# Hybrid decoder layer: where the decay factors of the SSD groups are formed, and where the memory tiles of the values are loaded and split

## The chip, the cores and the metric

The kernel runs as one program on one core of one Trainium2 chip. The metric is the device time of one execution in microseconds (us); the median of three runs is given.

## The reference

One decoder layer on x (512 positions, 1024 features) with a fixed memory of 256 rows, all in float32: a SwiGLU feed-forward network (hidden width 2816, weight 0.5), a hybrid mixer, cross-attention into the memory with 4 heads, a second feed-forward network, and a norm. The change lies in the mixer and at the beginning of the cross-attention. The mixer has a state-space (SSD) half of 16 heads in 4 groups, and a differential-attention half of 8 heads; both end in one output projection. Cut to what matters:

```python
z, xbc, dt_raw, q, k, v = split_sizes(h @ w_in, IN_SIZES)
xbc = silu(causal_dwconv(xbc, conv_w, conv_b)); xs, bs, cs = split(xbc)
la_cum = cumsum(dt * a) within chunks of 128 positions
decay = exp(where(causal, la_cum[l] - la_cum[s], -inf))
y_diag = einsum('bclsg,bclsgr,bcsgrp->bclgrp', cb, decay, xdt)   # cb = C B^T
y_off  = einsum('bclgn,bcgrpn,bclgr->bclgrp', cc, prev, exp(la_cum))
y = (y_diag + y_off + d_skip * xh) * silu(z)        # then a norm over each group
x = x + concat([y_ssd, y_attn]) @ w_out
v_mem = rms_norm(mem) @ w_cv                        # cross-attention's values
```

## The kernel before

**Products.** Each float32 product of this region is made of three matmuls on split operands: high by high, low by high, high by low. `load_w` loads a weight tile of 128 rows with a DMA on SP's queue (`wr`, 6 buffers), forms its high half on ACT (`wh`, line 155 in `split_into`) and its low half on DVE (`wl`, line 156); both have 3 buffers. PE can use a weight when ACT and then DVE have passed it.

**Order.** The class `Order` (`od`) sets the order in which the program is written. Its list of dense generators (`od.add`) yields after each product; beside them run chains, started by `od.spawn(gen, after)`. A chain goes on when the order's own time `od.t`, which each matmul advances by an assumed cost, has come to its due time; the table `W` (lines 38 to 40) holds the delays that a chain yields between its steps. On PE, DVE and ACT a scheduler puts the instructions in their final order from there; on SP and POOL the order of the program stands.

The dense list in the region is:

```python
    od.add(group_dense(0))
    od.add(out_attn(0, 0, 8))
    od.add(queries_keys(4))
    od.add(values(1))
    ...
    od.add(group_dense(2))
    od.add(group_dense(3))
    od.add(out_attn(1, SPLIT, 8, True))
    od.add(memory_values())
    od.add(out_proj(ys, a["wos"], ...))
```

**Groups.** `group_dense(g)` makes four convolved tiles of a group (products `pxbc`, then `conv` and gating `th2`), starts the chain `group`, and makes two gate tiles (`pz`). The chain of a group makes, with delays between: `pcb` and its masked copy `cbm`; the transpositions of the x tiles (`pxt`, then `xdt` and `xde` on DVE); those of B (`pbt`, copied to `btk` on ACT); the states (`pst`, `st`); and for each pair j of heads a decay block and the products that need it, `pf` (from the states) and `py` (from the decay). A decay block for (group, j) is, for each of two heads, one Exp of 64x512 (line 890), four Relu of 128x128 (892) and one Exp of 128x512 (893) on ACT and a product with `cbm` on DVE (894). It works in place on tiles that `decays` has loaded on ACT's queue; in the profile these are named `gate` for j = 0 and `th` for j = 1. The end of the chain gates with z, forms the norm (`pn` on PE, `nv` on DVE, `ncol` on POOL, `rh`, `ch` and `cl` on DVE), two diagonal tiles `ndiag` on POOL (line 368), their product `nrow`, and `y` (935), split into `ysh` and `ysl`.

**Beside them.** `queries_keys` and `values` make q, k and v of head attention (`pq`, `pk`, `pv`; the key tile is split into `kh` and `kl`). `out_attn` multiplies attention's result (`ya`) by the weights woa, 512 wide, into `pm`, which DVE adds to x. `memory_prep` loads eight tiles of the memory, 128x256, on SP's queue, and splits each (`hm`, line 159 on ACT and 160 on DVE); `memory_values` multiplies them by the weights wcv into four banks `pcv`.

Of the kernel before, what the change touches and what calls it, by code (L numbers as in the profile page):

```python
# [13 lines left out]
AF = mybir.ActivationFunctionType  # L14
ALU = mybir.AluOpType
# [20 lines left out]
LEAD = 4  # L36

W = {"h0": 3.4, "hs": 3.3, "hv": 2.08, "hp": 6.75}
W |= {"g0": 8.28, "gc": 0.75, "gx": 0.92, "gb": 2.59, "gs": 0.51, "gt": 2.0, "gd": 6.9, "gy": 0.38, "gq": 11.02, "gn": 6.52}
W |= {"v": 21.8, "c0": 4.97, "cs": 3.0, "ct": 4.82}  # L40

SPLIT, AHEAD = 5, 2
# [58 lines left out]
def body(tc, a, dbg=None):  # L101
# [13 lines left out]
    def nm(s):  # L115
        uid[0] += 1
        return f"{s}_{uid[0]}"

    def s2(s, dt=F32, shape=(P, T)):
        if math.prod(shape[1:]) <= T // 2:  # L120
            return sp.tile(list(shape), dt, tag="s1", name=nm(s), bufs=NHALF)
        return sp.tile(list(shape), dt, tag="s2", name=nm(s))
# [7 lines left out]
    def acc(s, shape=(P, T)):  # L130
        return acc_p.tile(list(shape), F32, tag="acc", name=nm(s))

    def aux(s, shape=(P, T)):
        return aux_p.tile(list(shape), F32, tag="aux", name=nm(s))
# [6 lines left out]
    V, S, G = nc.vector, nc.scalar, nc.gpsimd  # L141
    od = Order()
# [448 lines left out]
    def col64(s):  # L591
        return cp.tile([P, 4, 16], F32, name=s)

    cum, cdec, dend, dth = col64("cum"), col64("cdec"), col64("dend"), col64("dth")
# [176 lines left out]
        ya[hd] = split("ya", pt, wsub)  # L771
        dump(f"ya_{hd}", ya[hd][0])

    def out_attn(hg, o0, o1, prep=False):
        if prep:
            od.spawn(memory_prep(hm2, 1.5), 4.0)
        yield lambda: all(y is not None for y in ya[4 * hg : 4 * hg + 4])
        heads = ya[4 * hg : 4 * hg + 4]
        for o in range(o0, o1):
            po = acc("pm")  # L780
            yield from proj(po, load_w(a["woa"][hg, o], 4 * P), heads)
            V.tensor_tensor(x[o], x[o], po, ALU.add)
        if o1 == KT:
            ya[4 * hg : 4 * hg + 4] = [None] * 4
# [20 lines left out]
    ys = [None] * 8  # L805

    def group_dense(g):
        bc, xs, zs = [], [], []
        yield from xbc_tile(8 + g, bc)
        yield from xbc_tile(12 + g, bc)  # L810
        for j in range(2):
            yield from xbc_tile(2 * g + j, xs)
        od.spawn(group(g, bc[0], bc[1], xs, zs), W["g0"])
        for j in range(2):
            ps = acc("pz")
            yield from proj(ps, load_w(a["wz"][2 * g + j]), h)
            zs.append(silu2(ps))

    rows_of = {}
# [9 lines left out]
    def group(g, bt, ct, xs, zs):  # L829
        hsl = slice(4 * g, 4 * g + 4)  # L830

        def by_head(t):
            return t.rearrange("p c (h e) -> p c h e", e=64)


        pcb = aux("pcb", (P, 4, P))
        for c in range(4):
            mm(pcb[:, c], bt[:, c * P : (c + 1) * P], ct[:, c * P : (c + 1) * P], True, True)
        cbm = s2("cbm", shape=(P, 4, P))
        V.tensor_tensor(cbm, pcb, triq[:, None, :].to_broadcast([P, 4, P]), ALU.mult)  # L840
        yield W["gc"]
        xdt, xde = [], []
        for c2 in range(2):
            pt = aux("pxt", (P, 2, 256))
            for c in range(2):
                for j in range(2):
                    transpose(pt[:, c, j * P : (j + 1) * P], xs[j][:, (2 * c2 + c) * P : (2 * c2 + c + 1) * P])
            xd = s2("xdt", shape=(P, 2, 256))
            V.tensor_tensor(by_head(xd), by_head(pt), dth[:, 2 * c2 : 2 * c2 + 2, hsl, None].to_broadcast([P, 2, 4, 64]), ALU.mult)
            nc2 = 2 - c2  # L850
            xe = s2("xde", shape=(P, nc2, 256))
            V.tensor_tensor(by_head(xe), by_head(xd[:, :nc2]), dend[:, 2 * c2 : 2 * c2 + nc2, hsl, None].to_broadcast([P, nc2, 4, 64]), ALU.mult)
            xdt.append(xd)
            xde.append(xe)
            yield W["gx"]
        pb = aux("pbt", (P, 3, P))
        for c in range(3):
            transpose(pb[:, c], bt[:, c * P : (c + 1) * P])
        btk = s2("btk", shape=(P, 3, P))
        S.activation(btk, pb, AF.Copy)  # L860
        yield W["gb"]

        st = []
        for c in range(3):
            pst = aux("pst", (P, 256))
            mm(pst, btk[:, c], xde[c // 2][:, c % 2], True, True)
            sc = s2("st", shape=(P, 256))
            if c == 0:
                S.activation(sc, pst, AF.Copy)
            else:  # L870
                V.tensor_tensor(
                    sc.rearrange("p (h e) -> p h e", e=64),
                    st[-1].rearrange("p (h e) -> p h e", e=64),
                    cdec[:, c, hsl, None].to_broadcast([P, 4, 64]),
                    ALU.mult,
                )
                V.tensor_tensor(sc, pst, sc, ALU.add)
            st.append(sc)
            if c < 2:
                yield W["gs"]  # L880
        yz = []
        for j in range(2):
            rs = rows_of.pop((g, j))
            py = aux("py")
            e2 = s2("e2")
            for hh in range(2):
                hd = 4 * g + 2 * j + hh
                pp = slice(64 * hh, 64 * hh + 64)
                r = rs[hh]
                S.activation(e2[pp], r[pp].rearrange("p a b -> p (a b)"), AF.Exp)  # L890
                for c in range(4):
                    S.activation(r[:, c], r[:, c], AF.Relu, bias=cum[:, c, hd : hd + 1], scale=-1.0)
                S.activation(r, r, AF.Exp, scale=-1.0)
                V.tensor_tensor(r, r, cbm, ALU.mult)
            yield W["gd"] + (W["gt"] if j == 0 else 0.0)
            pf = aux("pf")
            with behind(list(newest_mm)):
                for c in range(1, 4):
                    mm(pf[:, c * P : (c + 1) * P], st[c - 1][:, j * P : (j + 1) * P], ct[:, c * P : (c + 1) * P], True, True)
                for c in range(4):  # L900
                    for hh in range(2):
                        pp = slice(64 * hh, 64 * hh + 64)
                        mm(py[pp, c * P : (c + 1) * P], xdt[c // 2][:, c % 2, (2 * j + hh) * 64 : (2 * j + hh + 1) * 64], rs[hh][:, c], True, True)
            if g < 3:
                decays(g + 1, j)
            dsk = dskh[:, 2 * g + j : 2 * g + j + 1]
            V.scalar_tensor_tensor(e2[:, P:], pf[:, P:], 0.5, e2[:, P:], ALU.mult, ALU.mult)
            y = s2("y")
            V.scalar_tensor_tensor(y, xs[j], dsk, py, ALU.mult, ALU.add)
            V.tensor_tensor(y[:, P:], y[:, P:], e2[:, P:], ALU.add)  # L910
            dump(f"y_{2*g+j}", y)
            yz.append(y)
            yield W["gy"]
        while len(zs) < 2:
            yield 1.0
        sq = []
        for j in range(2):
            V.tensor_tensor(yz[j], yz[j], zs[j], ALU.mult)
            q_ = s2("ysq")
            S.activation(q_, yz[j], AF.Square)  # L920
            sq.append(q_)
        G.tensor_tensor(sq[0], sq[0], sq[1], ALU.add)
        yield W["gq"]
        pn = aux("pn", (P, 4))
        for b in range(4):
            mm(pn[:, b : b + 1], sq[0][:, b * P : (b + 1) * P], ones[:, 0:1], True, True)

        rr = inv_rms_cols(pn, 4, 1.0 / (4 * 256), EPS)
        rh = small("rh", 4)
        V.tensor_scalar(rh, rr, 0.5, None, ALU.mult)  # L930
        yield W["gn"]
        pr = row_of(rh, 4, G, G)
        for j in range(2):
            n = 2 * g + j
            V.scalar_tensor_tensor(yz[j], yz[j], par[:, C_SSD + n : C_SSD + n + 1], pr, ALU.mult, ALU.mult)
            ys[n] = split("ys", yz[j])
            dump(f"ys_{n}", ys[n][0])
# [19 lines left out]
    def memory_prep(dst, apart=2.0):  # L957
        mem = [memory_tile(k) for k in range(KT)]
        for k, mk in enumerate(mem):
            with behind(recent):  # L960
                dst.append(split("hm", mk, par[:, C_MEM + k : C_MEM + k + 1], True))
            yield apart
# [69 lines left out]
    hm, hm2 = [], []  # L1032
# [13 lines left out]
    od.add(out_attn(1, 0, SPLIT))  # L1046
    od.add(group_dense(2))
    od.add(group_dense(3))
    od.add(out_attn(1, SPLIT, 8, True))
    od.add(memory_values())  # L1050
    od.add(out_proj(ys, a["wos"], lambda: all(y is not None for y in ys), upd_c))

# [351 lines left out]
```

## Time and profile before

| what | value |
|---|---|
| runs | 1333.7, 1337.35, 1333.83 us; median 1333.83 |
| profiled execution | 1333.16 us, span 1331.4 us |
| mean granted clock of TensorE | 0.996 |
| PE, PEld, DVE busy | 1305.6, 1136.6, 976.2 us |
| ACT, POOL busy | 663.0, 112.3 us |
| instructions | 20052 |

PE is TensorE's matmuls and PEld its weight loads; ACT is ScalarE, DVE is VectorE, POOL is GpSimd, and SP issues DMAs. A shape such as 128x512 is partitions by elements. In rows of the trace the first number is the start in us and the second the duration; "[5.67 <-ACT wh L155]" is idle time of that engine ahead of the instruction and what ended it. The engines and queues work side by side, so a busy engine costs time only where another waits for it.

### The profile page before, as it was taken

To read this page: it belongs to the slowest core of one execution; us is meant where nothing else is said; L and a number is where in the kernel's file an instruction comes from. 1 tells how busy PE (TensorE), PEld (TensorE's weight loads), DVE (VectorE), ACT (ScalarE), POOL (GpSimd) and SP (SyncE) were. 2 spreads that over 40 slices of the span, in tenths; PEclk is the share of its full clock that TensorE was granted. 3 is DMA by queue.
4 is the path that set the end of the run, shared out by engine and by line. 5 is a ranking of instruction groups with operands and counts; after the bars stand their busy time and mean duration, and the time that the engine had idled before them with its cause. 6 is when DMAs were issued, how large, how long until landed. Compare 5 with 4: busy or idle time off the path is not lost. (4 is left out here: it accounts for less than half of the span.)

```text
span 1331.4 us, 20052 instructions
## 1 busy us (share of the span) xinstructions
PE 1305.6 (98%) x7769; PEld 1136.6 (85%) x7769; DVE 976.2 (73%) x1528; ACT 663.0 (50%) x1114; POOL 112.3 (8%) x127
## 2 busy tenths in 40 slices
PE   8999999999999999999999989999999999999997
PEld 7898998899887778777788868888889999989995
DVE  6874778487885786647767776656678878887896
ACT  6442445154453564336644645434455545554564
POOL 0000010000010011200112021120001100000001
PEclk9999999999999999999999999999999999999999
DMA  7444577556464435763276477786239776666762
GB/s 271 111 127 127 127 198 246 134 145 172 128 234 151 126 87 128 225 200 99 60 208 197 109 205 225 200 208 173 61 114 244 205 224 175 190 193 174 194 200 95
DMA packets 67999, 222.71 MB, mean 167 GB/s; under 512 B 8424, under 2 KB 11984, under 8 KB 67552
## 3 DMA queue, kind: packets, MB, share of 16 engines
q1 hardware_dynamic: 52400, 174.42, 39.3%
q0 software_dynamic: 11904, 40.45, 17.1%
q10 hardware_dynamic: 3600, 6.56, 1.5%
q8 instruction: 61, 1.00, 0.3%
q14 instruction: 34, 0.28, 0.1%
HBM read 219.24 MB, written 50.91 MB: 203 GB/s over the span
## 5 line engine op out<-in xcount | busy, mean ns | idle before, releaser
L155 ACT ACTIVATE wh<-wr 128x1024 fp32r<-128x1024 f32 (+2 forms) x311 | 316.8, 1021 | 382.7 <-PE po L146 61.7
L156 DVE TENSOR_TENSOR wl<-wr,wh 128x1024 fp32r<-128x1024 f32 (+2 forms) x311 | 367.2, 1183 | 116.9 <-ACT wh L155 114.0
L146 PE MATMUL po<-gh,wh 128*128 128x512 f32 x176 | 68.8, 392 | 0.0
L146 PE MATMUL po<-gl,wh 128*128 128x512 f32 x176 | 68.5, 390 | 0.0
L146 PE MATMUL po<-gh,wl 128*128 128x512 f32 x176 | 68.4, 389 | 0.0
L240 PE MATMUL qa<-hml,wh 128*128 128x256 f32 x216 | 61.1, 283 | 0.0
L240 PE MATMUL qa<-hmh,wl 128*128 128x256 f32 x216 | 61.1, 283 | 0.0
L240 PE MATMUL qa<-hmh,wh 128*128 128x256 f32 x216 | 61.1, 283 | 0.0
L146 PE MATMUL pxbc<-hnh,wh 128*128 128x512 f32 x128 | 52.1, 407 | 0.0
L146 PE MATMUL pxbc<-hnl,wh 128*128 128x512 f32 x128 | 50.2, 392 | 0.0
L146 PE MATMUL pxbc<-hnh,wl 128*128 128x512 f32 x128 | 50.2, 392 | 0.0
L706 ACT ACTIVATE ec<-ec,mn 128x512 f32<-128x512 f32 (+3 forms) x64 | 35.5, 555 | 24.8 <-DVE mn L705 24.7
L511 DVE TENSOR_TENSOR upd<-po,row 128x512 f32<-128x512 f32 x24 | 16.6, 690 | 39.1 <-PE po L146 38.8
L240 PE MATMUL qe<-s31h,wl 128*128 128x256 f32 x152 | 43.2, 284 | 0.5 <-DVE wl L156 0.5
L240 PE MATMUL qb<-s24h,wl 128*128 128x256 f32 x152 | 43.1, 284 | 0.5 <-DVE wl L156 0.5
L240 PE MATMUL qe<-s31h,wh 128*128 128x256 f32 x152 | 43.1, 284 | 0.0
L240 PE MATMUL qe<-s24h,wh 128*128 128x256 f32 x152 | 43.0, 283 | 0.0
L240 PE MATMUL qb<-hmh,wh 128*128 128x256 f32 x152 | 43.0, 283 | 0.0
L240 PE MATMUL qb<-hml,wh 128*128 128x256 f32 x152 | 43.0, 283 | 0.0
L240 PE MATMUL qb<-hmh,wl 128*128 128x256 f32 x152 | 43.0, 283 | 0.0
L240 PE MATMUL qe<-s24h,wl 128*128 128x256 f32 x152 | 43.0, 283 | 0.0
L240 PE MATMUL qb<-s31h,wl 128*128 128x256 f32 x152 | 43.0, 283 | 0.0
(444 smaller groups left out, 4063.3 us busy)
## 6 DMA issues: line engine op xcount, KB each, us to landing
wr<-in_f2q SPq DMA_DIRECT2D x44, 512.0 KB, 4.4
wr<-in_f1q SPq DMA_DIRECT2D x40, 512.0 KB, 4.1
isum<-in_f2q SPq DMA_DIRECT2D x22, 512.0 KB, 5.7
wr<-isum SPq DMA_DIRECT2D x22, 512.0 KB, 4.4
wsum<-in_f2b SPq DMA_DIRECT2D x20, 512.0 KB, 6.2
wr<-wsum SPq DMA_DIRECT2D x20, 512.0 KB, 4.2
wr<-in_f1q POOLq DMA_DIRECT2D x16, 512.0 KB, 5.6
wr<-in_f1o SPq DMA_DIRECT2D x16, 512.0 KB, 4.0
```

What stands on the lines that cost most here:

```text
L146: newest_mm[:] = [nc.tensor.matmul(out, w, x, start=start, stop=stop).ins]
L155: S.activation(hi, src, AF.Copy),
L156: V.tensor_tensor(lo, src, hi.bitcast(F32), ALU.subtract),
L240: newest_mm[:] = [nc.tensor.matmul(out, a_[:, wc], b_, start=first and f == 0 and kp == 0 and j == 0, stop=kp == n - 1 and j == 2, skip_gr ...
L511: V.tensor_tensor(upd, po, row4, ALU.mult)
L706: S.activation(ec[:, :n], ec[:, :n], AF.Exp, bias=mn, scale=-1.0, accum_out=sm[c][:, i : i + 1])
```

## The change

Two things are changed, and no operation is added or taken out.

1. The decay block of a pair becomes a function `decayed(j)` in `group`. `decayed(0)` is called ahead of the transpositions, after the first delay ("gc"); `decayed(1)` after the states and a delay of 4.0 ("ga"). The products of pair 0 follow at once, where 8.9 (6.9 and 2.0) lay between states and products before; those of pair 1 follow after 6.9 ("gd").
2. `memory_prep` for the values is started at the beginning of `group_dense(3)`, due 18.0 later and with 2.0 between tiles, no longer at the beginning of the last `out_attn`, due 4.0 later with 1.5 between tiles.

```diff
--- before.py
+++ after.py
@@ -36,7 +36,7 @@
 LEAD = 4
 
 W = {"h0": 3.4, "hs": 3.3, "hv": 2.08, "hp": 6.75}
-W |= {"g0": 8.28, "gc": 0.75, "gx": 0.92, "gb": 2.59, "gs": 0.51, "gt": 2.0, "gd": 6.9, "gy": 0.38, "gq": 11.02, "gn": 6.52}
+W |= {"g0": 8.28, "gc": 0.75, "gx": 0.92, "gb": 2.59, "gs": 0.51, "ga": 4.0, "gd": 6.9, "gy": 0.38, "gq": 11.02, "gn": 6.52}
 W |= {"v": 21.8, "c0": 4.97, "cs": 3.0, "ct": 4.82}
 
 SPLIT, AHEAD = 5, 2
@@ -771,9 +771,7 @@
         ya[hd] = split("ya", pt, wsub)
         dump(f"ya_{hd}", ya[hd][0])
 
-    def out_attn(hg, o0, o1, prep=False):
-        if prep:
-            od.spawn(memory_prep(hm2, 1.5), 4.0)
+    def out_attn(hg, o0, o1):
         yield lambda: all(y is not None for y in ya[4 * hg : 4 * hg + 4])
         heads = ya[4 * hg : 4 * hg + 4]
         for o in range(o0, o1):
@@ -805,6 +803,8 @@
     ys = [None] * 8
 
     def group_dense(g):
+        if g == 3:
+            od.spawn(memory_prep(hm2, 2.0), 18.0)
         bc, xs, zs = [], [], []
         yield from xbc_tile(8 + g, bc)
         yield from xbc_tile(12 + g, bc)
@@ -838,7 +838,24 @@
             mm(pcb[:, c], bt[:, c * P : (c + 1) * P], ct[:, c * P : (c + 1) * P], True, True)
         cbm = s2("cbm", shape=(P, 4, P))
         V.tensor_tensor(cbm, pcb, triq[:, None, :].to_broadcast([P, 4, P]), ALU.mult)
+        e2s, rows = [], []
+
+        def decayed(j):
+            rs, e2 = rows_of.pop((g, j)), s2("e2")
+            for hh in range(2):
+                hd = 4 * g + 2 * j + hh
+                pp = slice(64 * hh, 64 * hh + 64)
+                r = rs[hh]
+                S.activation(e2[pp], r[pp].rearrange("p a b -> p (a b)"), AF.Exp)
+                for c in range(4):
+                    S.activation(r[:, c], r[:, c], AF.Relu, bias=cum[:, c, hd : hd + 1], scale=-1.0)
+                S.activation(r, r, AF.Exp, scale=-1.0)
+                V.tensor_tensor(r, r, cbm, ALU.mult)
+            e2s.append(e2)
+            rows.append(rs)
+
         yield W["gc"]
+        decayed(0)
         xdt, xde = [], []
         for c2 in range(2):
             pt = aux("pxt", (P, 2, 256))
@@ -879,20 +896,13 @@
             if c < 2:
                 yield W["gs"]
         yz = []
+        yield W["ga"]
+        decayed(1)
         for j in range(2):
-            rs = rows_of.pop((g, j))
+            rs, e2 = rows[j], e2s[j]
+            if j:
+                yield W["gd"]
             py = aux("py")
-            e2 = s2("e2")
-            for hh in range(2):
-                hd = 4 * g + 2 * j + hh
-                pp = slice(64 * hh, 64 * hh + 64)
-                r = rs[hh]
-                S.activation(e2[pp], r[pp].rearrange("p a b -> p (a b)"), AF.Exp)
-                for c in range(4):
-                    S.activation(r[:, c], r[:, c], AF.Relu, bias=cum[:, c, hd : hd + 1], scale=-1.0)
-                S.activation(r, r, AF.Exp, scale=-1.0)
-                V.tensor_tensor(r, r, cbm, ALU.mult)
-            yield W["gd"] + (W["gt"] if j == 0 else 0.0)
             pf = aux("pf")
             with behind(list(newest_mm)):
                 for c in range(1, 4):
@@ -1046,7 +1056,7 @@
     od.add(out_attn(1, 0, SPLIT))
     od.add(group_dense(2))
     od.add(group_dense(3))
-    od.add(out_attn(1, SPLIT, 8, True))
+    od.add(out_attn(1, SPLIT, 8))
     od.add(memory_values())
     od.add(out_proj(ys, a["wos"], lambda: all(y is not None for y in ys), upd_c))
```

The first place is ACT at the last woa weights and the first memory weights. In before, these rows run from the end of group 3's states to the split of the first wcv weight (`gate` is pair 0 of group 3):

```order
L155 ACTIVATE ysh_1597_7857<-y_1540_7584 128x512
L155 ACTIVATE ysh_1599_7862<-y_1551_7669 128x512
L890 ACTIVATE e2_1604_7872<-gate_1539_7580 64x512 x2
L892 ACTIVATE gate_1539_7580<-gate_1539_7580,cum_240 128x128 x5
L893 ACTIVATE gate_1539_7580<-gate_1539_7580 128x512
L892 ACTIVATE gate_1539_7580<-gate_1539_7580,cum_240 128x128 x3
L159 ACTIVATE hm_1613_7903<-mem_1605_7887,par_77 128x256
L893 ACTIVATE gate_1539_7580<-gate_1539_7580 128x512
L159 ACTIVATE hm_1614_7915<-mem_1606_7889,par_77 128x256
L155 ACTIVATE wh_1617_7922<-wr_1616_7920 128x512
L159 ACTIVATE hm_1619_7936<-mem_1607_7891,par_77 128x256
L155 ACTIVATE wh_1625_7949<-wr_1624_7947 128x1024
```

and after the change from the last gating of group 3 to the first two wcv weights:

```order
L788 ACTIVATE th2_1577_7766<-pz_1567_7718 128x512
L159 ACTIVATE hm_1582_7779<-mem_1553_7649,par_77 128x256
L159 ACTIVATE hm_1583_7795<-mem_1554_7651,par_77 128x256
L155 ACTIVATE wh_1622_7938<-wr_1621_7936 128x512
L849 ACTIVATE e2_1586_7805<-gate_1534_7555 64x512 x2
L851 ACTIVATE gate_1534_7555<-gate_1534_7555,cum_240 128x128 x5
L852 ACTIVATE gate_1534_7555<-gate_1534_7555 128x512
L851 ACTIVATE gate_1534_7555<-gate_1534_7555,cum_240 128x128 x3
L159 ACTIVATE hm_1590_7832<-mem_1555_7653,par_77 128x256
L852 ACTIVATE gate_1534_7555<-gate_1534_7555 128x512
L155 ACTIVATE wh_1633_7994<-wr_1632_7992 128x1024
L155 ACTIVATE wh_1636_8013<-wr_1635_8011 128x1024
```

The last woa split (`wh` of 128x512) moved from behind the decay block and two memory splits to a place ahead of the block, and most memory splits to places above it; the `ysh` splits of group 2 went from ahead of the block to places behind the first two wcv splits.

The second place is SP, at the weights of group 3 (wxbc, wz) and the last of woa. Before:

```order
L174 DMA wr_1546_7628<-in_wxbc 128x1024
L174 DMA wr_1557_7694<-in_wz 128x1024
L1155 DMA wsum12_273<-in_f2b1 128x1024
L174 DMA wr_1562_7729<-in_wz 128x1024
L174 DMA wr_1581_7806<-in_woa 128x512
L1155 DMA wsum13_274<-in_f2b1 128x1024
L174 DMA wr_1589_7836<-in_woa 128x512
L945 DMA mem_1605_7887<-in_memT 128x256
L945 DMA mem_1606_7889<-in_memT 128x256
L945 DMA mem_1607_7891<-in_memT 128x256
L945 DMA mem_1608_7893<-in_memT 128x256
L945 DMA mem_1609_7895<-in_memT 128x256
```

After:

```order
L1165 DMA wsum12_273<-in_f2b1 128x1024
L955 DMA mem_1548_7639<-in_memT 128x256
L955 DMA mem_1549_7641<-in_memT 128x256
L955 DMA mem_1550_7643<-in_memT 128x256
L955 DMA mem_1551_7645<-in_memT 128x256
L955 DMA mem_1552_7647<-in_memT 128x256
L955 DMA mem_1553_7649<-in_memT 128x256
L955 DMA mem_1554_7651<-in_memT 128x256
L955 DMA mem_1555_7653<-in_memT 128x256
L174 DMA wr_1560_7673<-in_wxbc 128x1024
L174 DMA wr_1568_7719<-in_wz 128x1024
L174 DMA wr_1579_7770<-in_wz 128x1024
```

The eight loads of the memory moved from between the second and the third woa weight to a place ahead of group 3's last wxbc and its two wz.

The third place is DVE in group 0, at the weights of wv (`wl` of 128x1024), the split of a query tile (`ql`) and of a key tile (`kl`), and the end of group 0's norm (`nv` to `cl`, on which POOL's two `ndiag` follow). Before:

```order
L156 TENSOR_TENSOR wl_1092_5720<-wr_1090_5717,wh_1091_5719 128x1024
L160 SCALAR_TENSOR_TENSOR ql_1071_5631<-pq_1066_5598,qh_1070_5630 128x512
L355 TENSOR_SCALAR nv_1078_5669<-pn_1077_5664 128x4
L930 TENSOR_SCALAR rh_1080_5673<-ncol_1079_5671 128x4
L362 CAST ch_1093_5727<-rh_1080_5673 128x4
L364 TENSOR_TENSOR cl_1094_5729<-rh_1080_5673,ch_1093_5727 128x4
L156 TENSOR_TENSOR wl_1104_5772<-wr_1102_5769,wh_1103_5771 128x1024
L156 TENSOR_TENSOR kl_1082_5679<-pk_1073_5636,kh_1081_5678 128x512
L156 TENSOR_TENSOR wl_1107_5803<-wr_1105_5800,wh_1106_5802 128x1024
L935 SCALAR_TENSOR_TENSOR y_1046_5487<-y_1046_5487,par_77,nrow_1095_5731 128x512
```

After:

```order
L156 TENSOR_TENSOR wl_1089_5690<-wr_1087_5687,wh_1088_5689 128x1024
L355 TENSOR_SCALAR nv_1071_5632<-pn_1070_5627 128x4
L940 TENSOR_SCALAR rh_1073_5636<-ncol_1072_5634 128x4
L362 CAST ch_1090_5696<-rh_1073_5636 128x4
L364 TENSOR_TENSOR cl_1091_5698<-rh_1073_5636,ch_1090_5696 128x4
L156 TENSOR_TENSOR wl_1101_5742<-wr_1099_5739,wh_1100_5741 128x1024
L160 SCALAR_TENSOR_TENSOR ql_1075_5642<-pq_1066_5598,qh_1074_5641 128x512
L156 TENSOR_TENSOR wl_1104_5772<-wr_1102_5769,wh_1103_5771 128x1024
L156 TENSOR_TENSOR kl_1082_5680<-pk_1077_5647,kh_1081_5679 128x512
L945 SCALAR_TENSOR_TENSOR y_1039_5461<-y_1039_5461,par_77,nrow_1092_5700 128x512
L945 SCALAR_TENSOR_TENSOR y_1055_5540<-y_1055_5540,par_77,nrow_1092_5700 128x512
```

The four small operations of the norm moved up by one weight split and the split of the query tile; two splits, not one, now stand between them and `wl` and `kl`.

## The prediction

> **What bounds the kernel now.** I read the page first: which engine is busy, at which clock, and which chain ended last.
>
> ```profile
> PE 1305.6 (98%) x7769; PEld 1136.6 (85%) x7769; DVE 976.2 (73%) x1528; ACT 663.0 (50%) x1114; POOL 112.3 (8%) x127
> ...
> PEclk9999999999999999999999999999999999999999
> ...
> PE 37%; DVE 1%; ACT 1%; issue 0%; POOL 0%; POOLq 0%; ACTq 0%
> ```
>
> PE is busy for 1305.6 of 1331.4 us, so 25.8 us are idle in all. Nearly all the steps of the chain are PE's; DVE and ACT have 1% each. The edit removes no matmul, so it can earn only PE's idle time and time at a reduced clock. Next I asked what PE waits for between 500 and 900 us, the stretch that the edit touches (columns: total us, times, longest).
>
> ```profile
> PE pm L146 <- ACT wh L155: 5.7, 1, 5.7
> PE pv L146 <- DVE kl L156: 2.2, 1, 2.2
> PE pt L150 <- DVE on L766: 1.3, 1, 1.3
> ...
> PE pq L146 <- ACT wh L155: 0.4, 1, 0.4
> ```
>
> Three stalls can go: A (5.7), C (2.2) and B (the 0.4, with one of the same size just behind it). The 1.3 stands in head attention, which the edit leaves alone. A first, with the busy time of PE, PEld, DVE, ACT and POOL, PE's granted clock and the DMA share by stretch, then PE's rows, and two rows of the chain (start, us, what).
>
> ```profile
> 780.00:800.00 20.00, 14.33 (x55) 11.13 (x53) 14.47 (x26) 11.97 (x26) 4.59 (x5) 0.85 0.74 187
> ...
> 796.00:798.00 2.00, 2.00 (x6) 1.51 (x6) 1.96 (x3) 1.75 (x4) 0.00 (x0) 0.50 0.72 193
> ...
> 788.66 0.39 PE L146 MATMUL pm<-yah,wl 128*128 128x512 f32 x1
> 794.71 0.79 PE L146 MATMUL pm<-yah,wh 128*128 128x512 f32 x1 [5.67 <-ACT wh L155]
> 800.00 0.63 PE L146 MATMUL pcv<-wh,hm 128*128 128x512 f32 x1
> ...
> 794.71 5.49 PE pm L146 x12
> ...
> 826.25 2.04 PE pm L146 x9
> ```
>
> A costs more than its wait. After 5.67 us of idleness the granted clock is 0.50, and the twelve products of the last woa tile stand from 794.71 to 800.00, 5.29 us. At the pace of undisturbed products in the last row, 2.04 / 9 = 0.227 us, they would take 2.72. The first memory products are still slow, which I put at 0.55 by their starts. So A costs 5.67 + 2.57 + 0.55 = 8.8 us. What was ACT doing? Its rows (with one of DVE for the splits), and SP's issue of that weight:
>
> ```profile
> 788.57 1.27 ACT L890 ACTIVATE e<-gate 64x512 f32<-64x512 f32 x2
> ...
> 791.85 0.97 ACT L892 ACTIVATE gate<-gate,cum 128x128 f32<-128x128 f32 x3
> 792.73 0.49 ACT L159 ACTIVATE hm<-mem,par 128x256 fp32r<-128x256 f32 x1
> ...
> 793.25 0.48 DVE L160 SCALAR_TENSOR_TENSOR hm<-mem,par,hm 128x256 fp32r<-128x256 f32 x1 [0.58 <-ACT hm L159]
> ...
> 794.05 0.61 ACT L155 ACTIVATE wh<-wr 128x512 fp32r<-128x512 f32 x1
> ...
> 770.57 0.38 SPq L174 DMA_DIRECT2D wr<-in_woa  x1
> ```
>
> The weight was issued 23 us earlier, so no transfer is late: ACT ran decay block (3,0) and two `hm` splits in front of the one `wh` that PE needed.
>
> B has the same pattern in group 0, with block (0,1) ahead of the splits:
>
> ```profile
> 543.06 0.39 PE L146 MATMUL pm<-yal,wh 128*128 128x512 f32 x1
> 543.86 0.50 PE L146 MATMUL pq<-hnh,wh 128*128 128x512 f32 x1 [0.41 <-ACT wh L155]
> 544.20 0.40 PE L146 MATMUL pq<-hnl,wh 128*128 128x512 f32 x1
> 544.98 0.50 PE L146 MATMUL pm<-yah,wl 128*128 128x512 f32 x1 [0.39 <-DVE wl L156]
> ...
> 537.53 1.29 ACT L890 ACTIVATE e<-th 64x512 f32<-64x512 f32 x2 [4.19 <-PE pm L146]
> ```
>
> By the starts, each gap exceeds a normal step: 0.80 - 0.23 and 0.78 - 0.23, together 1.1 us.
>
> C is of another kind, a DVE split beside two POOL operations:
>
> ```profile
> 561.86 3.45 DVE L156 TENSOR_TENSOR wl<-wr,wh 128x1024 fp32r<-128x1024 f32 x1
> 561.89 1.32 POOL L368 TENSOR_TENSOR ndiag<-ident,ch 128x512 fp32r<-128x512 f32 x1
> 562.90 1.31 POOL L368 TENSOR_TENSOR ndiag<-ident,cl 128x512 fp32r<-128x512 f32 x1
> 565.23 0.68 DVE L156 TENSOR_TENSOR kl<-pk,kh 128x512 fp32r<-128x512 f32 x1
> 565.96 0.50 PE L146 MATMUL pv<-wh,hnh 128*128 128x512 f32 x1 [2.18 <-DVE kl L156]
> ...
> 796.04 1.22 DVE L156 TENSOR_TENSOR wl<-wr,wh 128x1024 fp32r<-128x1024 f32 x1 [0.18 <-ACT wh L155]
> ```
>
> The same split takes 1.22 without POOL beside it; here it takes 3.45, 2.2 more, just PE's wait for the bank that `kl` frees. The two `ndiag` come from the group's norm, the end of its chain.
>
> **The change, part by part.** No instruction is added or removed; four decay blocks, the products behind them and eight memory loads move.
>
> *Group 0, B.* Block (0,0) goes ahead of the transpositions and block (0,1) behind the states. ACT then has both done by about 527 and 535, and nothing but splits stands before 544: gain 1.1. It could be 0 if (0,1) still met a split, but ACT was busy for only 9.87 of the 20 us from 510 (first of the next rows), so I take all of it.
>
> ```profile
> 510.00:530.00 20.00, 20.00 (x101) 16.79 (x100) 13.90 (x24) 9.87 (x23) 0.98 (x2) 1.00 0.68 166
> ...
> 763.00:782.00 19.00, 19.00 (x112) 16.14 (x111) 14.47 (x26) 7.54 (x14) 3.74 (x4) 1.00 0.66 197
> ```
>
> *Group 0, C.* Output products (0,0) come 4.9 earlier in the order's own time, and so does the whole end: `nv` stands one weight split earlier on DVE. The `ndiag` then run at about 554 to 557, beside the split of wv's second tile and `ql`, which PE needs only after the key tile. These stretch; the split and `kl` in front of the fourth pv bank do not. By my count `kl` then ends within 0.2 of the moment that PE reaches the bank, no longer 2.18 behind it: gain 2.1. Low end 0 (the stretch still delays `kl`), high end 2.2.
>
> *Groups 1 and 2* had no PE wait and keep slack: about 1.5 us at group 2's first outputs and 0.5 at the last xbc weight. I cost them at nothing, covered by PE's own products, at most 1 us if that cover is short.
>
> *Memory splits.* Eight `hm` splits, 0.49 on ACT and 0.48 on DVE each (3.9 on either), leave the place of A and run at 763 to 782, where ACT is busy for 7.54 of 19 and DVE for 14.47. ACT takes them freely; DVE comes near full: 14.47 + 3.9 = 18.4. What is late then is the gating of group 3's x tile, which stands on DVE behind `nv` and the splits; PE's transposition wants it at about 779.4, and I get 779.95: a new stall of 0.6 (0 to 1.5).
>
> *Their loads.* On SP the eight move ahead of group 3's last wxbc and two wz. Each queued DMA there waits for a semaphore lane and for its slot. Before, they held SP for long:
>
> ```profile
> 735.90 34.57 SPq L945 DMA_DIRECT2D mem<-in_memT  x8
> ...
> 711.98 0.34 SPq L174 DMA_DIRECT2D wr<-in_wxbc  x1
> ...
> 747.33 1.06 ACT L155 ACTIVATE wh<-wr 128x1024 fp32r<-128x1024 f32 x1 [0.17 <-PE pxbc L146]
> ...
> wr<-in_f2q SPq DMA_DIRECT2D x44, 512.0 KB, 4.4
> ```
>
> In the new place the slots that they take belong to head attention that ended before 700, and the lanes to DMAs of about 704; I expect SP to pass them by 712.5, against 711.98 before, and ACT takes that weight only at 747.33. Cost nothing; 35 us of lead, less the 4.4 of a landing (last row), is the cover.
>
> *Stall A.* The last woa tile's `wh` now stands ahead of block (3,0) on ACT. It waits only for its buffer, whose last reader is the end of pz:
>
> ```profile
> 781.60 0.40 PE L146 MATMUL pm<-yah,wh 128*128 128x512 f32 x1
> ...
> 786.59 1.41 DVE L935 SCALAR_TENSOR_TENSOR y<-y,par,nrow 128x512 f32<-128x512 f32 x2
> ...
> 788.25 1.28 DVE L156 TENSOR_TENSOR ysl<-y,ysh 128x512 fp32r<-128x512 f32 x2
> ```
>
> pz's end is the first pm's start, 781.60. PE wants that tile after 24 products, the norm's two row products and three transpositions, 24 x 0.227 + 1.1 = 6.6 later, at 788.2; `wh` and `wl` end by 784.2. So 4 us of slack, and the 8.8 us of A go, unless something takes their place. Next comes the first memory weight: `wh` behind block (3,0) (782.3 + 5.1, the 5.48 from 788.57 to 794.05 less one `hm`) ends at 788.5, but its `wl` stands on DVE behind two gate multiplications, two `y` (1.41), two x updates and one `ysl` (0.64), and I get 792.25. PE reaches the first product with it at 788.2 + 14 x 0.227 = 791.4: a new stall of 0.85 (0 to 3). State updates add 0.15. A nets 8.8 - 0.6 - 0.85 - 0.15 = 7.2 (4 to 8.8).
>
> Whether a leftover wait halves the clock decides its price. The trace: after 5.67 us idle 0.50, after C's 2.18 the clock stays full. The Trainium skill ("TensorE: Matmul & The Clock Gate", Part 1) puts the window at about 3.4 us. By it a leftover wait of 3.4 to 5 us would also cost some 3 us of slow products; my 0.6 and 0.85 lie below it either way.
>
> **Sum.** 7.2 + 1.1 + 2.1 = 10.4. Behind the memory products the order on PE is the old one, and PE has no slack to give the gain back to. The profiled execution took 1333.16 us (span 1331.4), so 1322.8; the median of the runs, 1333.83, is 0.67 above it, so 1323.4 against the median.
>
> **Rivals.**
> 1. *Part of it is eaten.* C stays (the `ndiag` meet another needed split) and the two new stalls reach 1.5 and 3. For it: DVE near 97% at 763 to 782. Against: no engine before PE is late by more than 1 us in my chain. Gain 8.8 - 4.6 + 1.1 = 5.3: 1328.5.
> 2. *The stall only moves one weight on.* Block (3,0) now stands before the first memory weight. If `wl` came 5 us late rather than 0.85, PE would idle as long as in A and halve its clock again: gain 3.2 of group 0 less 0.6, so 1331.2, no measurable change. For it: the same 5.5 us block on the same engine. Against: that weight is needed 3.2 us after the woa tile, and ACT starts the block 6 us earlier than before.
> 3. *Slower: the loads hold SP.* If the eight loads hold it from 704 as they did before (34.57), it is free at 738.6, and the weight lands 4.4 us later: just in time for 747.33. It decides from about 743 on; each later us is one of PE's idleness. Held until 757 (14 late) with some 3 us at half clock: 1333.2 - 10.4 + 14 + 3 = 1339.8, 1340.4 against the median. Against: slots and lanes free by 712.
> 4. *Contention moves rather than goes.* The `ndiag` of the other groups stretch a conv or gating DVE operation in front of a transposition, by up to C's 2.2 us, once: 1325.6. The Trainium skill ("SBUF — State Buffer", "Who interferes with whom") speaks for it: DVE with two SBUF inputs and POOL lock each other out of a port pair for whole instructions, wherever they meet. By it the new places count as much as the old; C's 3.45 against 1.22 agrees. Against it here: after the change each pair of `ndiag` stands beside work that PE wants more than 2 us later, by my count of the order.
>
> **How the numbers follow.** Main case 0.62, contention 0.13, partly eaten 0.12, only moved 0.07, slower 0.06. About 0.3%, 4.0 us, can be told from no change. Faster (1329.8 or less): the main case, contention, and nearly all of the partly eaten one, 0.86; same 0.08 (the moved stall and a rest); slower 0.06. The predicted time is the main case's, 1323.4. The range goes from the upper ends, 8.8 + 1.1 + 2.2 = 12.1, and the 1.3 of head attention, should its neighbours' shift remove it: 1320.4, up to 1329.5, which takes in the partly eaten case and leaves out 0.13 to 0.15.
>
> **What would show it.** PE's wait for `wh` at the last woa tile is gone and the granted clock stays 1.0 through 780 to 800; the waits for `wh` and `wl` near 544 and for `kl` near 566 are gone or under 0.3; new waits of PE on a gating operation of DVE (below 1.5) and on the first memory weight's `wl` (below 3). SP issues the eight `mem` within about 10 us. Wrong: a wait over 3.4 us on the memory weight with a clock of 0.5 behind it, or SP held in the `mem` rows past 743.

## The result, and the profile after

The changed kernel took 1321.37 us (median of 4 runs, 1320.8 to 1322.04), the kernel before 1333.82 us (four runs, three of them those of the table above); the ratio is 0.9903, with a 95% interval from 0.9891 to 0.9915. The forecast was 1323.4 us, in a range from 1320.4 to 1329.5, and faster with a chance of 0.86. The profiled execution of the changed kernel was the slowest of its four, 1322.04 us with a span of 1320.2, 11.2 below the span before.

First the busy time of the engines on the page after, then PE's waits between 500 and 900 us (total us, times, longest):

```profile
PE 1302.3 (99%) x7769; PEld 1135.3 (86%) x7769; DVE 976.1 (74%) x1528; ACT 664.0 (50%) x1114; POOL 111.7 (8%) x127
...
PE pt L150 <- DVE on L766: 1.3, 1, 1.3
PE pcv L146 <- DVE wl L156: 0.8, 1, 0.8
PE ps L146 <- DVE kl L156: 0.5, 1, 0.5
PE pxt L150 <- DVE th L789: 0.4, 1, 0.4
```

The 5.7, the 2.2 and the two 0.4 of group 0 are gone. New are the 0.8 and the 0.4. The busy time of DVE and ACT is the same: the work only stands elsewhere. PE's busy time fell by 3.3 us with the same 7769 matmuls, since none of them ran at the lower clock there any more. The stretches of the stalls show it (busy time of PE, PEld, DVE, ACT, POOL, then the granted clock and the DMA share):

```profile
540.00:560.00 20.00, 20.00 (x105) 16.64 (x104) 11.39 (x16) 6.05 (x8) 7.78 (x8) 1.00 0.79 265
560.00:580.00 20.00, 20.00 (x90) 16.36 (x89) 8.26 (x9) 5.82 (x7) 1.92 (x3) 1.00 0.87 242
780.00:800.00 20.00, 19.17 (x113) 15.46 (x112) 18.79 (x31) 16.45 (x34) 0.00 (x0) 1.00 0.49 155
```

In the last one DVE is busy for 18.79 of 20 us and ACT for 16.45, against 14.47 and 11.97 before: PE no longer stands here for 5.67 us and everything runs some microseconds earlier, so the same 20 us hold more work, and in part other work. Five rows of the timeline after tell why stall A is gone, and what took its place:

```profile
777.98 0.63 ACT L155 ACTIVATE wh<-wr 128x512 fp32r<-128x512 f32 x1 [0.54 <-PE pz L146]
778.51 1.27 ACT L849 ACTIVATE e<-gate 64x512 f32<-64x512 f32 x2
784.27 0.40 PE L146 MATMUL pm<-yah,wh 128*128 128x512 f32 x1
787.20 1.22 DVE L156 TENSOR_TENSOR wl<-wr,wh 128x1024 fp32r<-128x1024 f32 x1
788.47 0.50 PE L146 MATMUL pcv<-wl,hm 128*128 128x512 f32 x1 [0.83 <-DVE wl L156]
```

The last woa weight's high half is formed as soon as the last product of pz has freed its buffer, begun 6 us ahead of the tile that needs it, which PE starts at 784.27; the decay block follows behind it. The first memory weight's low half is 0.83 late. On SP the eight loads took 9.36 us, and the xbc weight behind them went out at once:

```profile
701.93 9.36 SPq L955 DMA_DIRECT2D mem<-in_memT  x8
711.39 0.38 SPq L174 DMA_DIRECT2D wr<-in_wxbc  x1
```

### The profile page after: what moved, and what is told of

The parts are those of the page before. It is cut to its first block, busy times and chain, and to the rows that moved or that the text cites. A ratio compares the mean times of both kernels' runs of the same rounds, so it can differ in the third digit from the quotient of the medians.

```text
span 1320.2 us, 20029 instructions
## 1 busy us (share of the span) xinstructions
PE 1302.3 (99%) x7769; PEld 1135.3 (86%) x7769; DVE 976.1 (74%) x1528; ACT 664.0 (50%) x1114; POOL 111.7 (8%) x127
## 4 chain that ended last, share of the span: by engine, by line
PE 87%; issue 6%; DVE 3%; ACT 1%; POOL 1%; DMA 1%; POOLq 0%; SPq 0%; ACTq 0%; DVEq 0%
PE qb L240 12%; PE po L146 10%; PE pm L146 9%; PE qe L240 7%; PE qa L240 7%; PE pxbc L146 7%; PE pcq L146 3%; PE ob L1199 3%; PE pz L146 3%; PE oa L1199 2%; PE pq L146 2%; PE oe L1199 2%; PE pk L146 2%; PE pa L146 2%; PE pcv L146 2%
## 5 line engine op out<-in xcount | busy, mean ns | idle before, releaser
L240 PE MATMUL qb<-s24h,wh 128*128 128x256 f32 x152 | 43.0, 283 | 0.0
L240 PE MATMUL qb<-s31l,wh 128*128 128x256 f32 x152 | 43.0, 283 | 0.0
```

The source lines that it names most:

```text
L240: newest_mm[:] = [nc.tensor.matmul(out, a_[:, wc], b_, start=first and f == 0 and kp == 0 and j == 0, stop=kp == n - 1 and j == 2, skip_gr ...
```

## The experiments

Theory: the decay blocks stood on ACT ahead of weight splits that PE wanted (A and B), POOL and DVE stood in each other's way (C), and a long wait of PE costs more than itself because the clock is halved behind it. Spans of profiled executions are compared with 1331.4 us before and 1320.2 after.

**The decay blocks alone.**

```diff
     def group_dense(g):
-        if g == 3:
-            od.spawn(memory_prep(hm2, 2.0), 18.0)
...
+    def out_attn(hg, o0, o1, prep=False):
+        if prep:
+            od.spawn(memory_prep(hm2, 1.5), 4.0)
...
+    od.add(out_attn(1, SPLIT, 8, True))
```

(against the changed kernel)

> Only the first part of the change: the decay blocks are formed where the changed kernel forms them, the memory tiles are loaded and split where the kernel before does it. Theory (the two parts overlap, each alone takes the last woa weight's high half out from behind a whole decay block): group 0 gains its 3.4 us as in the changed kernel (waits for wh, wl and kl near 544 and 566 gone), and at the last woa tile PE waits about 1 us (0 to 2.5), behind two hm splits and the first half of block (3,1), too short for the clock to halve. 1323.5 us (1322 to 1325.5). Rival (both parts are needed against stall A: two hm splits and a decay block still stand ahead of that weight): a wait of 4 to 6 us with a clock of 0.5 behind it, only group 0's gain is left, 1330.4 us.

1325.19 us, ratio 0.992 (0.9902 to 0.9937); span 1323.1. Its waits of PE from 700 to 830, four rows of the timeline, and the clock of one stretch:

```profile
PE pm L146 <- ACT wh L155: 2.7, 1, 2.7
...
783.01 1.27 ACT L849 ACTIVATE e<-th 64x512 f32<-64x512 f32 x2
...
785.79 0.61 ACT L852 ACTIVATE th<-th 128x512 f32<-128x512 f32 x1
786.89 0.61 ACT L155 ACTIVATE wh<-wr 128x512 fp32r<-128x512 f32 x1
787.55 0.50 PE L146 MATMUL pm<-yah,wh 128*128 128x512 f32 x1 [2.73 <-ACT wh L155]
...
790.00:792.00 2.00, 2.00 (x8) 1.72 (x8) 0.67 (x1) 0.35 (x1) 0.00 (x0) 0.50 0.72 221
```

The time lies at the upper end of what the theory gave, but not by its account. Group 0's waits are gone, and stall A shrank by half; yet 2.7 us are left, more than the 2.5 that I allowed, behind the splits and most of block (3,1), and the clock was halved for 3.4 us behind them. This part alone gives 8.3 of the 11.2 us.

**The memory splits alone.**

```diff
     def group_dense(g):
+        if g == 3:
+            od.spawn(memory_prep(hm2, 2.0), 18.0)
...
-    od.add(out_attn(1, SPLIT, 8, True))
+    od.add(out_attn(1, SPLIT, 8))
```

(against the kernel before)

> Only the second part: the memory tiles are loaded and split beside the last gates, the decay blocks stand where the kernel before has them. Theory (overlap): the waits of group 0 stay (0.4, 0.4 and 2.2 us), stall A goes with its half clock, with new waits of up to 1 us near the transpositions of group 3: 1326 us (1324.8 to 1327.5). Rival (block (3,0) still stands ahead of a weight that PE needs, and the stall moves to a memory weight): a wait over 3.4 us and a clock of 0.5 behind it, 1332 to 1334 us. SP holds the eight loads for about 10 us as in the changed kernel; if they were the cost of the change it would show here as a wait of PE for group 3's weights.

1329.03 us, ratio 0.9951 (0.9936 to 0.9966); span 1327.3. Stall A is gone altogether: between 770 and 850 PE waits for 0.8 (`cl` of a norm) and 0.2. So this part alone removes A, and the other removes about half of it; the savings of the two, 8.3 and 4.1, make 12.4, more than the 11.2 of both together, since each claims a part of A. The starts of products that all four kernels have, near 703 and 860 in the kernel before, show it without what lies elsewhere: between them the first part alone gains 4.9 us, the second 6.3, and both together 8.0. SP held the eight loads for 8.78 us. But the time misses the range that I gave, 1324.8 to 1327.5: the span fell by 4.1 us where I expected some 8. A part of that has a reason that I had not expected. Stall C had its 2.18 us again, but what came behind differs from the kernel before:

```profile
565.79 0.54 PE L146 MATMUL pv<-wh,hnh 128*128 128x512 f32 x1 [2.18 <-DVE kl L156]
...
566.00:568.00 2.00, 2.00 (x6) 1.59 (x6) 0.00 (x0) 0.00 (x0) 0.51 (x1) 0.53 0.95 152
568.00:570.00 2.00, 2.00 (x8) 1.54 (x7) 0.00 (x0) 0.00 (x0) 0.00 (x0) 0.62 1.28 433
```

The kernel before has in the first of these stretches:

```profile
566.00:568.00 2.00, 2.00 (x9) 1.63 (x10) 0.00 (x0) 0.00 (x0) 0.67 (x1) 1.00 1.02 161
```

The same wait, once with a clock of 1.00 behind it and once with 0.53: six products in 2 us against nine. The products behind it start 1.4 us later than those of the kernel before. With that, the 0.8 and A's gain, the account holds up to the first memory products, which start 6.0 us ahead of the kernel before. By the last of them 5.0 are left; the list of waits shows only 0.2 of that loss, and the rest stays open. Another 0.8 is lost near 1025 us, behind a wait of PE for ACT at line 299, far from the change; the second profile of the kernel before, further down, has such a wait too.

**Group 0's diagonals on ACT**, in the kernel before.

```diff
-            eng.tensor_tensor(diag, ident[...], c[...], ALU.mult)
+            if on_act:
+                for b in range(nb):
+                    S.activation(diag[:, b], ident, AF.Copy, scale=c[:, b : b + 1])
+            else:
+                eng.tensor_tensor(diag, ident[...], c[...], ALU.mult)
...
-        pr = row_of(rh, 4, G, G)
+        pr = row_of(rh, 4, G, G, g == 0)
```

> The kernel before, with the two ndiag of group 0 formed on ACT (eight operations of 128x128) instead of POOL; nothing else moves on DVE. Theory (stall C is DVE and POOL in each other's way): the split of wv's third tile takes 1.2 to 1.3 us and not 3.45, PE's wait for kl goes from 2.18 to 0 to 0.2, time 1331.6 us (1331.0 to 1332.2). Rival (that split is slow for another reason, a transfer into the same memory or its weight): it still takes over 3 us, the wait stays at about 2.2, 1333.8 us.

1330.67 us, ratio 0.997 (0.996 to 0.9981); span 1331.1. The split and `kl` of the timeline:

```profile
563.62 1.23 DVE L156 TENSOR_TENSOR wl<-wr,wh 128x1024 fp32r<-128x1024 f32 x1
563.88 1.27 ACT L370 ACTIVATE ndiag<-ident,ch 128x128 fp32r<-128x128 f32 x4
564.77 0.69 DVE L156 TENSOR_TENSOR kl<-pk,kh 128x512 fp32r<-128x512 f32 x1
565.05 1.27 ACT L370 ACTIVATE ndiag<-ident,cl 128x128 fp32r<-128x128 f32 x4
```

The split takes 1.23, not 3.45, and PE's wait of 2.18 for `kl` is gone. So the two `ndiag` on POOL made C. The products behind it gain 2.3 us on the kernel before, as the theory has it. The sizes of the whole do not follow: the medians differ by 4.0 us, more than the 1.6 to 2.8 that I gave, and the profiled span is only 0.3 below the kernel before. The span has a reason that lies elsewhere: in this execution the first products were slower for longer (12 of them from 8 to 12 us, 19 in the kernel before), and by 12 us it was 1.7 us behind. For the medians I have none; the clock behind C, which the run above found halved once, may be a part. Three rows of the changed kernel show that the change only put the contention elsewhere:

```profile
555.54 1.04 POOL L368 TENSOR_TENSOR ndiag<-ident,ch 128x512 fp32r<-128x512 f32 x1 [0.49 <-DVE ch L362]
555.60 2.06 DVE L156 TENSOR_TENSOR wl<-wr,wh 128x1024 fp32r<-128x1024 f32 x1
556.54 2.01 POOL L368 TENSOR_TENSOR ndiag<-ident,cl 128x512 fp32r<-128x512 f32 x1
```

Here a split of an earlier weight stretches to 2.06 and one `ndiag` to 2.01, where PE wants neither yet. The Trainium skill ("SBUF — State Buffer", "Who interferes with whom") has the two engines lock each other out for whole instructions. The trace agrees: the first `ndiag`, which started 0.06 ahead of the split, takes its usual 1.04; the split ends 1.08 behind it, and the second `ndiag` 0.89 behind the split.

**The memory splits earlier**, in the changed kernel.

```diff
-            od.spawn(memory_prep(hm2, 2.0), 18.0)
+            od.spawn(memory_prep(hm2, 2.0), 14.0)
```

> The changed kernel with the memory splits due 4 us earlier (14 instead of 18). Theory (the wait of 0.4 us at the transpositions of group 3 comes from the splits on DVE beside the last convolution, the wait of 0.8 at the first memory weight from the norm's end and ysl ahead of it): the first wait goes to 0 to 0.2, the second stays within 0.5 of 0.8, 1321.0 us (1319.8 to 1322.2), no difference that can be measured. Rival (loads that come earlier take slots or lanes that are not free, and hold SP): SP stands in the eight loads for over 15 us, PE waits for a weight of group 3, slower by 2 us or more.

1325.54 us, ratio to the kernel before 0.9928 (0.9913 to 0.9943), 3 to 4 us slower than the changed kernel, where I expected no difference. A wait came, but not through SP, which stood only 9.88 us in the loads:

```profile
746.98 1.27 ACT L849 ACTIVATE e<-th 64x512 f32<-64x512 f32 x2
748.27 1.57 ACT L851 ACTIVATE th<-th,cum 128x128 f32<-128x128 f32 x5
...
751.81 0.49 ACT L159 ACTIVATE hm<-mem,par 128x256 fp32r<-128x256 f32 x1
...
752.87 2.94 ACT L155 ACTIVATE wh<-wr 128x1024 fp32r<-128x1024 f32 x3
...
753.97 0.50 PE L146 MATMUL pxbc<-hnh,wh 128*128 128x512 f32 x1 [3.41 <-ACT wh L155]
...
756.00:758.00 2.00, 2.00 (x5) 1.56 (x6) 2.00 (x4) 1.03 (x2) 0.00 (x0) 0.50 0.66 169
```

It is stall A once more, one group earlier: block (2,1), a memory split and a convolution ahead of a weight's high half on ACT, 3.41 us of waiting and a clock of 0.50 behind it. The changed kernel has the same block and convolution there, but forms one more high half ahead of them:

```profile
737.66 1.06 ACT L155 ACTIVATE wh<-wr 128x1024 fp32r<-128x1024 f32 x1
```

So it is that split's place in the order, more than the memory split's 0.49, that made the wait. My third rival of the prediction, the loads, was the wrong thing to fear; the second, the stall that only moves, is what four units of the order's time bring about.

**A wait of chosen length.** In the changed kernel PE waits at the sixth memory tile for a copy on POOL, behind three or six fills.

```diff
+            if k == 5:
+                scr, late = s2("scr"), s2("late", R32, (P, MEM))
+                G.tensor_copy(scr[:, :4], x[7][:, :4])
+                for _ in range(3):          # or 6
+                    G.memset(scr, 0.0)
+                G.tensor_copy(late, hm2[k][0])
+                hm2[k] = (late, hm2[k][1])
```

> The changed kernel with an added wait of PE: the high half of the sixth memory tile is copied once more on POOL, behind three fills of a scratch tile and the last addition to x, so that PE must wait at that tile and no other engine is held for PE's sake. Theory (a wait of PE costs its length, and where it holds an idle stretch of some 2 to 3 us the granted clock may halve for some 3.5 us, according to where the stretch falls): a wait of 1.5 to 3.5 us, with the clock behind it either at 1.0 or at 0.5; time 1321.4 plus the wait, plus 1.7 if the clock halves. Rival (a fixed length between 2.2 and 2.7 us decides): the clock halves if the wait is above 2.7 and never below 2.2.

> The same with six fills in place of three. Theory: a wait of 3.5 to 6 us; the clock is at 0.5 for 3 to 7 us behind it in any case, and the time grows by the wait and 1.5 to 3.5 us more. Rival (what halved the clock behind stall A was not PE's idleness but something else at that place): the clock stays at 1.0, the time grows by the wait alone.

The waits were shorter than I had aimed at. Three fills, then six:

```profile
808.22 0.50 PE L146 MATMUL pcv<-wh,late 128*128 128x512 f32 x1 [1.09 <-POOL late L1007]
...
808.00:810.00 2.00, 1.78 (x8) 1.47 (x9) 0.73 (x4) 0.00 (x0) 2.00 (x4) 1.00 1.02 176
```

```profile
810.75 0.50 PE L146 MATMUL pcv<-wh,late 128*128 128x512 f32 x1 [2.84 <-POOL late L1007]
...
812.00:814.00 2.00, 2.00 (x6) 1.52 (x6) 0.27 (x2) 0.00 (x0) 2.00 (x3) 0.50 0.93 344
```

The wait of 1.09 left the clock at 1.00 (1323.84 us; a second wait of 1.1 for a low half came with it). Behind that of 2.84 it was halved; the span grew by 4.6 us, 1.8 more than the wait (1326.58 us). Nothing of A's surroundings is at this place, and three fills on POOL alone did not do it, so PE's idleness is the likely cause; each is a single execution. Neither length tells the theory from its rival, a fixed length between 2.2 and 2.7; the 2.18 that went both ways speaks against the rival.

**The kernel before, once more.**

> The kernel before, unchanged, profiled once more. Theory: the waits are the same to 0.1 us (5.7, 2.2, 0.4, 0.4); behind stall A the clock is 0.5 again; behind stall C (2.2) and over the first ten microseconds it may differ from the first profile, and the span differs by what the clock makes of it, up to 3 us. Rival (the clock behind a given wait is the same in each execution): C is followed by a clock of 1.0 again, the span is 1331.4 to within 0.5.

1332.48 us, span 1330.7. The waits are those of the first profile, C's clock is 1.00 again, and A's is not what it was:

```profile
794.00:796.00 2.00, 1.53 (x4) 1.13 (x5) 1.82 (x5) 2.00 (x4) 0.00 (x0) 0.50 0.00 0
796.00:798.00 2.00, 2.00 (x8) 1.59 (x7) 2.00 (x3) 1.51 (x3) 0.00 (x0) 0.67 0.96 299
798.00:800.00 2.00, 2.00 (x11) 1.65 (x10) 1.85 (x4) 1.06 (x1) 0.00 (x0) 1.00 0.89 311
```

The half clock lasted until about 797 and not 801, and cost 1.4 us instead of 3.1 at the last woa tile and the first memory products. The price of A is thus 7.1 to 8.8 us by that count; what sets it in an execution is not shown.

**The changed kernel once more, and the splits closer together.**

```diff
-            od.spawn(memory_prep(hm2, 2.0), 18.0)
+            od.spawn(memory_prep(hm2, 1.5), 18.0)
```

> The changed kernel, unchanged, timed beside the next one and profiled once more. Theory (it has no wait near 2 us left at which the clock could halve by chance): the waits are those of its first profile to 0.1 us (0.4 at the transpositions of group 3, 0.8 at the first memory weight), the clock is 1.0 behind them; ratio to the kernel before 0.989 to 0.992. Rival: a wait of 0.8 can be followed by a halved clock as well, the span is up to 2 us longer.

> The changed kernel with 1.5 instead of 2.0 between the memory splits, so that the last of them leaves the stretch ahead of the first memory weight. In its order PE now puts group 3's states and first output products ahead of the first product with that weight's low half. Theory (the wait of 0.8 was for a low half that came too soon on PE): that wait goes to 0 to 0.3; in its place PE may wait up to 1 us for btk, which stands on ACT behind two weight splits and two ysh; 1320.5 to 1322 us, no difference to the changed kernel that can be measured. Rival (btk or the states come 2 us late): a wait over 2 us, with the clock halved behind it, 3 us slower than the changed kernel.

The changed kernel: 1321.46 us (1321.32 to 1321.69), ratio 0.991 (0.9893 to 0.9926), with the waits of its first profile:

```profile
PE pcv L146 <- DVE wl L156: 0.8, 1, 0.8
PE pxt L150 <- DVE th L789: 0.4, 1, 0.4
```

With the splits closer: 1319.5 us (1319.46 to 1319.96), ratio 0.9895 (0.9881 to 0.991). Between 760 and 830 PE has no listed wait at all, `btk` was not late, and the span is 1317.7, 1.8 less. I had expected no difference that can be measured, 1320.5 at the least: the waits of 0.8 and 0.4 both went, and a little more. This version is faster than both kernels; on the same chip the slowest of its four runs lies 1.36 us below the fastest of the changed kernel's.

## Why the prediction was right

*The sum.* 10.4 us were forecast; the spans give 11.2, the medians 12.45. Where they were gained I read from the starts of the same product before and after. Group 0: 3.2 forecast (1.1 and 2.1); ahead of it the changed kernel is 0.5 behind, and behind the fourth pv bank 3.2 ahead, so 3.8 (1.4 and 2.4). The 0.5 comes from places that the edit leaves alone: 0.3 gained in the first microseconds and 0.8 lost between 202 and 209 us. Stall A with what took its place, from 703 to 860: 7.2 forecast, 8.0 measured. Half of the difference is what the half clock cost: I put it at 2.57 and 0.55, but the whole stretch, without PE's waits, is 3.5 us shorter after the change. The rest are new waits smaller than forecast. So both parts were put too low by some 0.6 to 0.8, and that the 0.5 elsewhere hides part of it is luck. The new waits: 0.85 and 0.6 forecast, 0.83 and 0.37 measured, and none for the 0.15 of the state updates. The rest up to 12.45 is in the runs: the changed kernel's profiled execution, 1322.04, was the slowest of four, and that of the kernel before, 1333.16, lies below all its timed runs.

*SP.* About 10 us for the eight loads were forecast, 9.36 measured, the xbc weight at 711.39 where 712.5 was forecast. The slow rival came in no run.

*Stall C.* The cause was right, and the term near (2.1 for 2.4). That contention would move and not go is also what the fourth rival says; it moved to a split with slack, as the main case has it, and PE waits for nothing there. The query split `ql` was not stretched as forecast: it took 0.68.

*The term least understood* is the price of a wait. I wrote that the clock stays full after 2.18 us; that was one execution. By all runs: at 0.83, 1.09 and 1.1 us, and at head attention's 1.3 in every profile, it stayed at 1.00; at 2.18 it stayed in two profiles and halved in one; at 2.73, 2.84, 3.41 and 5.7 it halved. The rule of the Trainium skill ("TensorE: Matmul & The Clock Gate", Part 1), an idle window of about 3.4 us, is too lenient here: PE was idle for only 2.18 to 2.84 us in three cases, and the clock was halved. That its window runs freely, so that chance decides, agrees with 2.18 us going both ways and with A's two prices. This decided nothing in the forecast, as the leftover waits lie below 1 us; it is a part of why two expectations of the experiments were too low (1323.5 for 1325.19 and 1326 for 1329.03).

*Slack at group 2.* Costed at nothing, rightly: from the fourth pv bank to 703 us the lead changes by less than 0.1. But it hung by little: with the memory splits four units earlier, a weight's high half fell behind block (2,1) on ACT, and 3.41 us came back.

## What to carry to other kernels

Work that nobody waits for yet, on an engine that also feeds PE, belongs behind the splits that PE wants next or a whole stage ahead of them; the cost of the wrong place here was the wait and, from 2.18 us on in some executions and from 2.73 on in all, 1.5 to 3.5 us more in slow products. When two edits aim at one stall, run each alone: here their savings overlapped, and one of them brought gains elsewhere. A delay in an order is worth trying on both sides: 14 instead of 18 cost 3 to 4 us, and a spacing of 1.5 instead of 2.0 gained 2.

## What had not been expected

The same wait of 2.18 us was followed by a clock of 1.00 in two executions and of 0.53 for 2 us in a third; behind A's 5.67 the half clock lasted for 3.4 us in one execution and for 6.8 in two others. Slices of half a microsecond show where it begins and ends, here after 2.73 us (the decay blocks alone) and after 5.67 (the kernel before):

```profile
788.50:789.00 0.50, 0.50 (x3) 0.35 (x3) 0.50 (x1) 0.50 (x1) 0.00 (x0) 0.76 0.00 0
792.00:792.50 0.50, 0.50 (x5) 0.38 (x6) 0.04 (x1) 0.00 (x0) 0.00 (x0) 0.83 0.64 238
...
794.00:794.50 0.50, 0.00 (x0) 0.00 (x0) 0.50 (x2) 0.50 (x2) 0.00 (x0) 0.55 0.00 0
800.50:801.00 0.50, 0.50 (x3) 0.40 (x2) 0.50 (x2) 0.37 (x1) 0.00 (x0) 0.62 1.03 385
```

A slice with a share between 0.5 and 1 holds a change of the clock, and the share tells where in it. The first pair gives 3.4 us from 788.8 to 792.2, begun 1.2 us after PE had started again; the second 6.8, from 794.05 to 800.9, begun 0.7 ahead of PE's start. In all seven half-clock stretches that follow one of these waits the length is 3.4 us or twice that, and nothing between; 3.4 us of it cost 1.5 to 2.0 us, 6.8 cost 3.2 and 3.5. So here the cost went in steps and not with the length of the wait.

Single executions of one kernel therefore differ by one or two microseconds without a difference in any wait. A kernel with none of these stalls varied less: 1319.46 to 1319.96 in four runs, where the kernel before went from 1332.12 to 1334.28 beside it.
